# A hybrid SSD and forgetting-attention block: h forms read from a float32 copy in memory, the softplus chain moved behind later slab pairs, the output gate in eight 1024-column steps

## The chip, the cores and the metric

The kernel runs on one core of a Trainium2 chip. Its five engines run their own instruction streams: TensorE (PE; PEld is its weight load), VectorE (DVE), ScalarE (ACT), GpSimd (POOL) and SyncE (SP), which here only issues DMAs. The metric is the device time of one launch in microseconds, as the median of several runs; lower is better.

## What is computed

One layer of a decoder trunk, sequence 1024, width 1024, in float32. What matters here, cut from the reference:

```python
ada = jax.nn.silu(c) @ w_ada + b_ada
shift, scale, gate = jnp.split(ada, 3, axis=-1)
h = _rmsnorm(x, norm_w) * (1.0 + scale) + shift
proj = jnp.einsum("bsd,de->bse", h, w_in)          # 8472 columns
z_ssm, xbc, dt_raw, q, k, v, z_att, f_logit, g_logit = jnp.split(proj, offsets, axis=-1)
dt = jax.nn.softplus(dt_raw + dt_bias)             # used by the SSD branch
a_cs = jnp.cumsum(dt * -exp(a_log), chunkwise)     # used by the SSD branch
f_cum = jnp.cumsum(log_sigmoid(f_logit + b_f))     # used by the attention branch
merged = g_ssm * (y_ssm @ w_proj_ssm) + g_att * (y_att @ w_proj_att)
x = x + gate * (merged @ w_out)
return _rmsnorm(x, final_norm_w)
```

## The kernel before

Every large product is made in three passes: each operand is split into a high and a low part (`split`, lines 98 and 99: a cast on ScalarE and a subtraction on VectorE), and TensorE adds high x high, high x low and low x high in PSUM. The work runs in stages.

1. **h.** x is normalised, transposed on TensorE and scaled by the adaLN columns into `xa` (ScalarE, line 301), 16 halves of 128x512. Each half is split into `hh` and `hl` (lines 302, 303). The adaLN columns come from 8 steps `ada_cols`, whose sums are VectorE's. The weights `w_ada`, x and the first units of the projection are loaded by SyncE's queue in that time.
2. **First slabs.** Three gate slabs, then `v_slab(0)` (four units of `w_v0`; its evacuation also copies the 24 columns of dt and f into `tmp`), then one more gate slab, `gate_slab(3)`.
3. **t forms.** Later slabs are projected in pairs by a seven-product (Strassen-like) scheme, `c_pair`. Four of the products take sums of h rather than h. `t_forms(k)`, k = 0 to 3, makes these: it adds `hh` and `hl` back to float32 (line 436, four adds for each k), makes four differences (lines 437 to 440) and splits them into `tha`, `tla`, `thb`, `tlb`.
4. **Softplus chain.** `dt_chain` turns `tmp` into dt and the logs of the forget gates; `ssm_sums` makes the running sums for the SSD branch. Their results go to memory (`f_scr`, `a_scr`, `e_scr`) and are read in stages 6 and 7.
5. **Pairs.** A loop over `PAIRS`, 19 slab pairs of 7 x 12 matmuls. `WPREP[n]` says what is prepared ahead of pair n for the end of the kernel: sums of the weights of the two output projections (`w_sums`, 'ps', 'pa', 'o') and the output gate. The gate is `silu(c) @ w` by VectorE: `out_gate` multiplies blocks of weights by columns of silu(c) and adds them in `gb` (lines 558 and 561), `gate_sum` adds over partitions with a matmul against ones (line 570).
6. **SSD** with the remaining slabs as filler, 7. **attention**, 8. **output projections** and the last norm.

The code's order isn't the engines' order: a scheduler sorts each engine's instructions by priorities and a simulated timeline when the kernel is built, and then each engine runs its list strictly in order. Buffers come from pools with few slots: `wr` (raw weights, 4 slots), `pe` (4), `sh` (4), and `ev` (4 slots of 128x1028, shared by nearly all that goes to memory).

Of the kernel before, what the change touches and what calls it, by code (L numbers as in the profile page):

```python
# [31 lines left out]
P = 128  # L32
# [19 lines left out]
WPREP = {0: [('ps', 0)], 2: [('ps', 1)], 3: [('ps', 2)], 6: [('ps', 3), ('pa', 0)], 8: [('pa', 1)], 10: [('pa', 2), ('g', 0)], 12: [('pa', 3), ('g', 2), ('g', 3)], 11: [('g', 1)], 13: [('G', 0)], 15: [('o', 0)], 16: [('o', 1)], 17: [('o', 2)], 18: [('o', 3)]}  # L52
# [13 lines left out]
def build(ctx, tc, t):  # L66
# [98 lines left out]
    m_scr = {}  # L165
    z_scr = [dram.tile([P, S], F32, name=f"z_scr{j}") for j in range(8)]
# [31 lines left out]
    with tc.tile_pool(name="st", bufs=1, side="right") as st, \  # L198
# [95 lines left out]
        def h_half(k, hf):  # L294
# [6 lines left out]
            A.activation(out=xa, in_=tp, func=AF.Identity, scale=av[:, k:k + 1], bias=sv[:, k:k + 1])  # L301
            A.copy(out=hh[k][:, fs], in_=xa)  # L302
# [24 lines left out]
    ed = const.tile([P, NC, 8], F32, name="ed")  # L327

# [27 lines left out]
    with tc.tile_pool(name="pa", bufs=1, side="right") as pa, \  # L356
            tc.tile_pool(name="pap", bufs=1, space=PSUM) as pap:

        def dt_chain(dtf, tmp):
# [21 lines left out]
            lf = tmp[:, 192:256].rearrange("p (h c) -> p h c", h=8)  # L381
            pre = tmp[:, 256:320].rearrange("p (h c) -> p h c", h=8)
# [3 lines left out]
            for c in range(1, 8):  # L386
                V.tensor_tensor(out=pre[:, :, c:c + 1], in0=pre[:, :, c - 1:c], in1=lf[:, :, c - 1:c], op=ALU.add)
            ps = pap.tile([P, 512], F32, tag="pp", bufs=5, name="pp")
            PE.matmul(ps[0:64, 0:P], lhsT=tmp[:, 192:256], rhs=tri, start=True, stop=False)
            PE.matmul(ps[0:64, 0:P], lhsT=tmp[:, 256:320], rhs=ones, start=False, stop=True)  # L390
            ft = tmp[0:64, 320:320 + P]
            V.tensor_copy(out=ft, in_=ps[0:64, 0:P])
            SP.dma_start(out=f_scr, in_=ft)

            V.tensor_copy(out=dt, in_=v[:, :, 0:16])
# [35 lines left out]
        def t_forms(k):  # L431
            th1, tl1, th2, tl2 = (pa.tile([P, S], F32R, name=f"t{n}{k}") for n in ("ha", "la", "hb", "lb"))
            b11, b12, b21, b22 = (pe_tile() for _ in range(4))
            lo, hi = slice(0, 512), slice(512, 1024)
            for b, kk, hs, eng in ((b11, k, lo, V), (b12, k, hi, V), (b22, k + 4, hi, V), (b21, k + 4, lo, V)):
                eng.tensor_tensor(out=b, in0=f32(hh[kk][:, hs]), in1=f32(hl[kk][:, hs]), op=ALU.add)
# [812 lines left out]
```

## Time and profile before

| what | value |
|---|---|
| median of 3 runs | 1234.88 us (1232.15 to 1235.67) |
| profiled execution: its time | 1229.0 us |
| profiled execution: its span | 1227.2 us |
| busy share of PE, PEld, DVE, ACT, POOL | 95%, 79%, 79%, 51%, 7% |
| mean granted TensorE clock | 0.992 |
| DMA | 219.67 MB, mean 179 GB/s |

The profiled execution is one execution; its time is 0.5% under the median of the others, and its span lies 1.8 us under its own time. A busy share is an average over the stages. TensorE is nearly always busy, so what costs time is where its row has a gap, and what ended that gap.

### The profile page before, as it was taken

What the parts mean: (1) busy time and instruction counts of PE and PEld (TensorE: products, weight loads), DVE (VectorE), ACT (ScalarE), POOL (GpSimd) and SP (SyncE); (2) the same over time, 40 slices, a digit from 0 to 9 for tenths busy, and PEclk for the clock granted to TensorE, in tenths of its full rate; (3) what the DMA queues carried; (4) which work ended last, traced back from release to release, by engine and by line L of the source; (5) the groups of instructions that cost most, each with busy time, mean ns of one, the idle gap of its engine ahead of it and who ended that gap; (6) DMA issues with size and microseconds to landing.
All of it is one profiled execution on the core that took longest, in us unless ns stands there. A gap on an engine that the chain in (4) does not pass through costs nothing.

```text
span 1227.2 us, 18314 instructions
## 1 busy us (share of the span) xinstructions
PE 1162.5 (95%) x6206; PEld 975.1 (79%) x6206; DVE 969.8 (79%) x1990; ACT 626.2 (51%) x1252; POOL 87.2 (7%) x152
## 2 busy tenths in 40 slices
PE   4999899999999999999999989999988998999997
PEld 3797688778877788998888768888877886788875
DVE  6879687887987785589999987664677968989967
ACT  5555344353442344777776633453456654454455
POOL 2000000000000000000000002222322220000001
PEclk9999999999999999999999989999999999999999
DMA  8442442655384756546646658422246526955333
GB/s 350 178 155 98 165 164 79 229 188 190 115 291 167 243 206 223 207 134 205 207 149 199 205 185 304 157 88 89 87 162 208 182 77 239 334 181 180 103 95 146
DMA packets 104122, 219.67 MB, mean 179 GB/s; under 512 B 11818, under 2 KB 19420, under 8 KB 103004
## 3 DMA queue, kind: packets, MB, share of 16 engines
q1 hardware_dynamic: 104028, 218.50, 52.8%
q8 instruction: 49, 0.80, 0.3%
q14 instruction: 45, 0.37, 0.1%
HBM read 154.85 MB, written 63.61 MB: 178 GB/s over the span
## 4 chain that ended last, share of the span: by engine, by line
PE 71%; DVE 14%; DMA 8%; issue 3%; ACT 3%; POOL 0%; SPq 0%; POOLq 0%; DVEq 0%; ACTq 0%
PE pp L492 6%; PE pp L495 6%; PE pp L494 6%; PE pv L1054 4%; PE mm L492 4%; PE mm L494 4%; PE mm L495 4%; PE lg L1023 3%; PE mm L112 3%; PE mm L111 3%; PE mm L113 3%; DMA ab<-a_scr 2%; PE tp L1044 2%; PE mm L908 2%; PE mm L906 2%
## 5 line engine op out<-in xcount | busy, mean ns | idle before, releaser
L98 ACT CAST wh<-wr 128x512 fp32r<-128x512 f32 (+1 forms) x214 | 130.4, 620 | 159.6 <-PE mm L494 27.9
L99 DVE TENSOR_TENSOR wl<-wr,wh 128x512 fp32r<-128x512 f32 (+1 forms) x214 | 145.8, 689 | 47.3 <-ACT wh L98 46.1
L112 PE MATMUL mm<-hl,wh 128*128 128x512 f32 x288 | 116.9, 406 | 0.0
L111 PE MATMUL mm<-hh,wh 128*128 128x512 f32 x288 | 115.5, 406 | 0.1
L113 PE MATMUL mm<-hh,wl 128*128 128x512 f32 x288 | 114.7, 399 | 0.0
L138 PE MATMUL mm<-wh,hl 128*128 128x256 f32 (+1 forms) x256 | 73.7, 289 | 0.0
L136 PE MATMUL mm<-wh,hh 128*128 128x256 f32 (+1 forms) x256 | 73.2, 288 | 0.0
L137 PE MATMUL mm<-wl,hh 128*128 128x256 f32 (+1 forms) x256 | 73.1, 286 | 0.0
L1029 ACT ACTIVATE pr<-pr,sm 128x1024 f32<-128x1024 f32 (+3 forms) x64 | 50.0, 781 | 44.9 <-DVE sm L1028 38.0
L1047 ACT CAST pth<-tp 128x512 fp32r<-128x512 f32 (+1 forms) x80 | 42.4, 542 | 52.7 <-PE tp L1044 44.1
L1024 DVE CUSTOM_DVE_ANT_0 pr<-lg,fb 128x512 f32<-128x512 f32 (+1 forms) x96 | 51.6, 552 | 17.8 <-PE lg L1023 12.2
L112 PEld LDWEIGHTS mm<-hl,wh 128*128 128x128 f32 x288 | 54.9, 191 | 10.8 <-DVE hl L303 0.9
L111 PEld LDWEIGHTS mm<-hh,wh 128*128 128x128 f32 x288 | 54.5, 191 | 10.9 <-ACT hh L302 0.9
L113 PEld LDWEIGHTS mm<-hh,wl 128*128 128x128 f32 x288 | 54.8, 190 | 10.1
L683 ACT ACTIVATE ab<-ab,acs 128x128 f32<-128x128 f32 x128 | 41.0, 391 | 36.5 <-DMA ab<-a_scr 32.7
L1032 POOL TENSOR_SCALAR pr<-pr,sm 128x1024 f32<-128x1024 f32 (+3 forms) x64 | 52.0, 813 | 83.1 <-DVE sm L1031 65.9
L1048 DVE TENSOR_TENSOR ptl<-tp,pth 128x512 fp32r<-128x512 f32 (+1 forms) x80 | 49.9, 631 | 10.0 <-ACT pth L1047 9.7
L789 POOL TENSOR_TENSOR rc<-rc,mhalf 128x8 f32<-128x8 f32 x1 | 1.6, 1647 | 703.9 <-DVE rc L787 703.9
L1054 PE MATMUL pv<-pth,vh 128*128 128x256 f32 (+1 forms) x160 | 45.2, 282 | 4.9 <-DVE zg L1057 4.0
L98 ACT CAST sh<-sr 128x512 fp32r<-128x512 f32 x57 | 34.0, 620 | 30.3 <-PE pp L494 15.0
L137 PEld LDWEIGHTS mm<-wl,hh 128*128 128x128 f32 x256 | 48.2, 189 | 0.2
L138 PEld LDWEIGHTS mm<-wh,hl 128*128 128x128 f32 x256 | 48.2, 189 | 0.1
(399 smaller groups left out, 3507.6 us busy)
## 6 DMA issues: line engine op xcount, KB each, us to landing
wr<-w_c SPq DMA_DIRECT2D x116, 256.0 KB, 3.4
wa<-w_ada SPq DMA_DIRECT2D x8, 1024.0 KB, 11.4
g_scr<-gt SPq DMA_DIRECT2D x16, 512.0 KB, 4.1
ab<-a_scr SPq DMA_DIRECT2D x32, 256.0 KB, 3.6
gt<-g_scr SPq DMA_DIRECT2D x32, 256.0 KB, 3.9
wr<-w_ps SPq DMA_DIRECT2D x28, 256.0 KB, 2.9
wr<-w_pa SPq DMA_DIRECT2D x28, 256.0 KB, 2.8
wr<-so SPq DMA_DIRECT2D x28, 256.0 KB, 2.7
```

What stands on the lines that cost most here:

```text
L98: A.copy(out=hi[:, :n], in_=raw[:, :n])
L99: eng.tensor_tensor(out=lo[:, :n], in0=raw[:, :n], in1=f32(hi[:, :n]), op=ALU.subtract)
L111: PE.matmul(ps, lhsT=hi[:, cs], rhs=xh[k][:, hs], start=(k == 0), stop=False)
L112: PE.matmul(ps, lhsT=hi[:, cs], rhs=xl[k][:, hs], start=False, stop=False)
L113: PE.matmul(ps, lhsT=lo[:, cs], rhs=xh[k][:, hs], start=False, stop=(k == 7))
L136: PE.matmul(o, lhsT=xh[k][:, ts], rhs=hi[:, cs], start=(k == 0), stop=False)
L137: PE.matmul(o, lhsT=xh[k][:, ts], rhs=lo[:, cs], start=False, stop=False)
L138: PE.matmul(o, lhsT=xl[k][:, ts], rhs=hi[:, cs], start=False, stop=(k == 7))
L492: PE.matmul(ps, lhsT=f[0][:, w], rhs=xh[:, hs], start=(first and k == 0), stop=False, skip_group_check=True)
L494: PE.matmul(ps, lhsT=f[0][:, w], rhs=xl[:, hs], start=False, stop=False, skip_group_check=True)
L495: PE.matmul(ps, lhsT=f[1][:, w], rhs=xh[:, hs], start=False, stop=(k == 3), skip_group_check=True)
L1054: PE.matmul(pv[:, o0:256], lhsT=x[kb // 4][:, kb % 4, vs], rhs=y[:, d:d + m], start=(kb == 0 and i == 0), stop=(kb == 2 * qq + 1 and i == 2))
```

## The change

Six edits. The 16 halves of `xa` are also stored to memory (`h_scr`); `t_forms` loads its four float32 blocks from there rather than adding `hh` and `hl`, for odd k into slots of `sh` rather than `pe`. `gate_slab(3)` now stands ahead of `t_forms`. The 24 columns in `tmp` go to memory (`d_scr`), come back at pair 2, where `dt_chain` now is; its two matmuls (`f_sums`) and `ssm_sums` stand at pair 5. The first `ps` step of `WPREP` moves from pair 0 to pair 1. `out_gate` takes whole rows of 1024 columns, two of the eight k each time, in place of 256 columns for all eight. A constant tile `fl` holds what `tmp` held of the f part (and later `rc`).

```diff
-WPREP = {0: [('ps', 0)], 2: [('ps', 1)], 3: [('ps', 2)], 6: [('ps', 3), ('pa', 0)], 8: [('pa', 1)], 10: [('pa', 2), ('g', 0)], 12: [('pa', 3), ('g', 2), ('g', 3)], 11: [('g', 1)], 13: [('G', 0)], 15: [('o', 0)], 16: [('o', 1)], 17: [('o', 2)], 18: [('o', 3)]}
+WPREP = {1: [('ps', 0)], 2: [('ps', 1)], 3: [('ps', 2)], 6: [('ps', 3), ('pa', 0)], 8: [('pa', 1)], 10: [('pa', 2), ('g', 0)], 12: [('pa', 3), ('g', 2), ('g', 3)], 11: [('g', 1)], 13: [('G', 0)], 15: [('o', 0)], 16: [('o', 1)], 17: [('o', 2)], 18: [('o', 3)]}
...
+    h_scr = [dram.tile([P, S], F32, name=f"h_scr{k}") for k in range(NK)]
+    d_scr = dram.tile([P, 192], F32, name="d_scr")
...
             A.activation(out=xa, in_=tp, func=AF.Identity, scale=av[:, k:k + 1], bias=sv[:, k:k + 1])
+            SP.dma_start(out=h_scr[k][:, fs], in_=xa)
             A.copy(out=hh[k][:, fs], in_=xa)
             V.tensor_tensor(out=hl[k][:, fs], in0=xa, in1=f32(hh[k][:, fs]), op=ALU.subtract)
...
+    fl = const.tile([P, P], F32, name="fl")
...
-            lf = tmp[:, 192:256].rearrange("p (h c) -> p h c", h=8)
-            pre = tmp[:, 256:320].rearrange("p (h c) -> p h c", h=8)
+            lf = fl[:, 0:64].rearrange("p (h c) -> p h c", h=8)
+            pre = fl[:, 64:128].rearrange("p (h c) -> p h c", h=8)
...
+            V.tensor_copy(out=dt, in_=v[:, :, 0:16])
+
+        def f_sums():
             ps = pap.tile([P, 512], F32, tag="pp", bufs=5, name="pp")
-            PE.matmul(ps[0:64, 0:P], lhsT=tmp[:, 192:256], rhs=tri, start=True, stop=False)
-            PE.matmul(ps[0:64, 0:P], lhsT=tmp[:, 256:320], rhs=ones, start=False, stop=True)
-            ft = tmp[0:64, 320:320 + P]
-            V.tensor_copy(out=ft, in_=ps[0:64, 0:P])
-            SP.dma_start(out=f_scr, in_=ft)
-
-            V.tensor_copy(out=dt, in_=v[:, :, 0:16])
+            PE.matmul(ps[0:64, 0:P], lhsT=fl[:, 0:64], rhs=tri, start=True, stop=False)
+            PE.matmul(ps[0:64, 0:P], lhsT=fl[:, 64:128], rhs=ones, start=False, stop=True)
+            V.tensor_copy(out=fl[0:64], in_=ps[0:64, 0:P])
+            SP.dma_start(out=f_scr, in_=fl[0:64])
 
...
         def t_forms(k):
             th1, tl1, th2, tl2 = (pa.tile([P, S], F32R, name=f"t{n}{k}") for n in ("ha", "la", "hb", "lb"))
-            b11, b12, b21, b22 = (pe_tile() for _ in range(4))
+            b11, b12, b21, b22 = (pe_tile() if k % 2 == 0 else pa.tile([P, 512], F32, tag="sh", bufs=SB[1], name="sb")
+                                  for _ in range(4))
             lo, hi = slice(0, 512), slice(512, 1024)
-            for b, kk, hs, eng in ((b11, k, lo, V), (b12, k, hi, V), (b22, k + 4, hi, V), (b21, k + 4, lo, V)):
-                eng.tensor_tensor(out=b, in0=f32(hh[kk][:, hs]), in1=f32(hl[kk][:, hs]), op=ALU.add)
+            for b, kk, hs in ((b12, k, hi), (b11, k, lo), (b22, k + 4, hi), (b21, k + 4, lo)):
+                SP.dma_start(out=b, in_=h_scr[kk][:, hs])
             V.tensor_tensor(out=b11, in0=b12, in1=b11, op=ALU.subtract)
             V.tensor_tensor(out=b12, in0=b22, in1=b12, op=ALU.subtract)
             V.tensor_tensor(out=b22, in0=b22, in1=b11, op=ALU.subtract)
...
             gb = ev("gb") if gb is None else gb
-            gc = slice(g * 256, (g + 1) * 256)
-            for hf in range(2):
-                wa = ev("wga")[:, :1024].rearrange("p (k c) -> p k c", k=4)
-                SP.dma_start(out=wa, in_=t["w_gate"][g, hf])
-                for kk in range(4):
-                    k = hf * 4 + kk
-                    if k == 0:
-                        V.tensor_scalar(out=gb[:, gc], in0=wa[:, kk, :], scalar1=cols[:, k:k + 1], scalar2=None,
-                                        op0=ALU.mult)
-                    else:
-                        V.scalar_tensor_tensor(out=gb[:, gc], in0=wa[:, kk, :], scalar=cols[:, k:k + 1],
-                                               in1=gb[:, gc], op0=ALU.mult, op1=ALU.add)
+            for k in (2 * g, 2 * g + 1):
+                wa = ev("wga")[:, :D]
+                SP.dma_start(out=wa, in_=t["w_gate"][k])
+                if k == 0:
+                    V.tensor_scalar(out=gb[:, :D], in0=wa, scalar1=cols[:, k:k + 1], scalar2=None, op0=ALU.mult)
+                else:
+                    V.scalar_tensor_tensor(out=gb[:, :D], in0=wa, scalar=cols[:, k:k + 1], in1=gb[:, :D],
+                                           op0=ALU.mult, op1=ALU.add)
             return gb
...
         tmp = ev("tmp")
         dtf = tmp[:, 0:192].rearrange("p (c n) -> p c n", n=24)
         v_slab(0, dtf)
+        SP.dma_start(out=d_scr, in_=tmp[:, 0:192])
+        gate_slab(3)
         for k in range(4):
             t_forms(k)
-        gate_slab(3)
-        dt_chain(dtf, tmp)
-        ssm_sums()
         gb = None
         for n, (sa, sb) in enumerate(PAIRS):
+            if n == 2:
+                tmp = ev("tmp")
+                SP.dma_start(out=tmp[:, 0:192], in_=d_scr)
+                dt_chain(tmp[:, 0:192].rearrange("p (c n) -> p c n", n=24), tmp)
+            if n == 5:
+                f_sums()
+                ssm_sums()
             for wn, p in WPREP.get(n, ()):
                 if wn == "g":
...
-        rc = const.tile([P, 8], F32, name="rc")
+        rc = fl[:, 0:8]
...
-        "w_gate": _ada_groups(i["w_ada"][:, 2048:3072].reshape(1024, 1, 1024)),
+        "w_gate": np.ascontiguousarray(i["w_ada"][:, 2048:3072].reshape(8, 128, 1024)),
```

How the engines' lists move, at the three places that the prediction speaks of.

VectorE, from the last halves of h on (line 303, now 306). Before, the adds of line 436 follow at once, four for each k:

```order
L303 TENSOR_TENSOR hl_245<-xa,hh_237 128x512 x2
L303 TENSOR_TENSOR hl_246<-xa,hh_238 128x512 x2
L436 TENSOR_TENSOR pe<-hh_231,hl_239 128x512 x2
L436 TENSOR_TENSOR pe<-hh_235,hl_243 128x512 x2
L437 TENSOR_TENSOR pe<-pe 128x512
L438 TENSOR_TENSOR pe<-pe 128x512
L99 TENSOR_TENSOR wl<-wr,wh 128x560
L439 TENSOR_TENSOR pe<-pe 128x512
L99 TENSOR_TENSOR wl<-wr,wh 128x512
L99 TENSOR_TENSOR tla_1063<-pe,tha_1062 128x512
L440 TENSOR_TENSOR pe<-pe 128x512
L436 TENSOR_TENSOR pe<-hh_232,hl_240 128x512
```

Now (lines 442 to 445 are the four differences; `sb` are the slots of `sh`):

```order
L306 TENSOR_TENSOR hl_254<-xa,hh_246 128x512 x2
L306 TENSOR_TENSOR hl_255<-xa,hh_247 128x512 x2
L442 TENSOR_TENSOR pe<-pe 128x512
L99 TENSOR_TENSOR wl<-wr,wh 128x560
L443 TENSOR_TENSOR pe<-pe 128x512
L99 TENSOR_TENSOR wl<-wr,wh 128x512
L444 TENSOR_TENSOR pe<-pe 128x512
L442 TENSOR_TENSOR sb<-sb 128x512
L99 TENSOR_TENSOR tla_1156<-pe,tha_1155 128x512
L445 TENSOR_TENSOR pe<-pe 128x512
L99 TENSOR_TENSOR tla_1156<-pe,tha_1155 128x512
L443 TENSOR_TENSOR sb<-sb 128x512
```

The adds are gone, and the first instruction after h is a difference of two loaded blocks.

SyncE's queue at the same place. Before (line 85: units of a slab; 579: `w_ps`; 183: a gate slab to memory):

```order
L85 DMA wr<-w_v 128x560 x4
L85 DMA wr<-w_c 128x512 x2
L579 DMA wr<-w_ps 128x512
L183 DMA g_scr_95<-gt 128x1024
L579 DMA wr<-w_ps 128x512
L183 DMA g_scr_96<-gt 128x1024
L579 DMA wr<-w_ps 128x512
L183 DMA g_scr_97<-gt 128x1024
L579 DMA wr<-w_ps 128x512
```

Now (line 304: the stores of xa; 441: the loads of `t_forms`; 463: raw weights of a pair):

```order
L85 DMA wr<-w_c 128x512
L463 DMA wr<-w_c 128x512
L304 DMA h_scr_184<-xa 128x512 x2
L304 DMA h_scr_185<-xa 128x512 x2
L304 DMA h_scr_186<-xa 128x512 x2
L441 DMA pe<-h_scr_179 128x512 x2
L441 DMA pe<-h_scr_183 128x512 x2
L441 DMA sb<-h_scr_180 128x512 x2
L441 DMA sb<-h_scr_184 128x512 x2
L185 DMA g_scr_95<-gt 128x1024
L463 DMA wr<-w_c 128x512
L185 DMA g_scr_96<-gt 128x1024
```

The last stores of h and the first eight loads stand ahead of the gate slabs' stores, and pair 0's raw weights ahead of `w_ps`. The first of the loads into `pe` waits, in the built program, for the stores of h to have completed.

TensorE at the gate's sum (line 570, now 571). Before, the first of its two matmuls stands in the middle of a pair, and the second 50 matmuls later:

```order
L494 MATMUL pp<-tlb_1137,wh 128x512
L495 MATMUL pp<-thb_1136,wl 128x512
L570 MATMUL pp<-gb,ones 128x512
L492 MATMUL pp<-tha_1062,sh 128x512
L494 MATMUL pp<-tla_1063,sh 128x512
```

Now both stand side by side, at the end of a pair and ahead of the next:

```order
L497 MATMUL pp<-hh_247,sh 128x512
L499 MATMUL pp<-hl_255,sh 128x512
L500 MATMUL pp<-hh_247,sl 128x512
L571 MATMUL pp<-gb,ones 128x512
L571 MATMUL mm<-gb,ones 128x512
L497 MATMUL mm<-hh_240,wh 128x512
```

From the start of TensorE's list, the two stood as its 1551st and 1601st matmul, and now as its 1563rd and 1564th; each column of `gb` is now complete only after the last of the eight steps.

## Rows read from the trace of the kernel before

**Rows 1.** The page: busy time by engine, and the chain by engine.
```profile
PE 1162.5 (95%) x6206; PEld 975.1 (79%) x6206; DVE 969.8 (79%) x1990; ACT 626.2 (51%) x1252; POOL 87.2 (7%) x152
...
PE 71%; DVE 14%; DMA 8%; issue 3%; ACT 3%; POOL 0%; SPq 0%; POOLq 0%; DVEq 0%; ACTq 0%
```

**Rows 2.** Windows 70:110 and 110:134.
```profile
core 0: us, PE busy (x) PEld busy (x) DVE busy (x) ACT busy (x) POOL busy (x), PEclk, DMA share, GB/s
70.00:110.00 40.00, 40.00 (x259) 37.15 (x258) 38.88 (x73) 21.32 (x41) 0.00 (x0) 1.00 0.49 165
110.00:134.00 24.00, 19.19 (x80) 14.21 (x79) 20.57 (x45) 9.45 (x17) 0.00 (x0) 1.00 0.48 163
```

**Rows 3.** TensorE in order of time, 110 to 140: its waits.
```profile
120.88 0.50 PE L492 MATMUL mm<-tha,wh 128*128 128x512 f32 x1 [1.46 <-ACT pe L506]
...
124.88 0.50 PE L492 MATMUL mm<-thb,wh 128*128 128x512 f32 x1 [0.96 <-ACT pe L509]
...
128.50 0.50 PE L492 MATMUL mm<-hh,sh 128*128 128x512 f32 x1 [0.57 <-DVE mm L513]
...
133.83 0.49 PE L405 MATMUL pp<-a,tri 128*128 128x128 f32 x2 [1.67 <-DVE a L400]
```

**Rows 4.** Window 60:125, line 436 alone (VectorE busy).
```profile
60.00:125.00 65.00, 10.37 (x16) 1.00 0.36 122
```

**Rows 5.** VectorE in order of time, at two places.
```profile
345.62 0.47 DVE L561 SCALAR_TENSOR_TENSOR gb<-wga,cols,gb 128x256 f32<-128x256 f32 x1
346.01 0.69 DVE L473 TENSOR_TENSOR sr<-wr 128x512 f32<-128x512 f32 x1
346.62 0.48 DVE L561 SCALAR_TENSOR_TENSOR gb<-wga,cols,gb 128x256 f32<-128x256 f32 x1
...
166.38 2.47 DVE L541 SCALAR_TENSOR_TENSOR cv<-xp,cols,cv 128x1024 f32<-128x1024 f32 x2
168.77 0.68 DVE L99 TENSOR_TENSOR wl<-wr,wh 128x512 fp32r<-128x512 f32 x1
```

**Rows 6.** ScalarE in order of time, the last xa.
```profile
68.23 0.78 ACT L301 ACTIVATE xa<-tp,sv,av 128x512 f32<-128x512 f32 x1 [1.10 <-PE tp L298]
```

**Rows 7.** DMA issues: count, KB each, median us to landing.
```profile
wr<-w_c SPq DMA_DIRECT2D x116, 256.0 KB, 3.4
...
sps<-sr SPq DMA_DIRECT2D x12, 256.0 KB, 3.3
...
wr<-w_v SPq DMA_DIRECT2D x4, 280.0 KB, 7.2
```

**Rows 8.** TensorE in order of time, gate slab 3 begins.
```profile
97.06 0.39 PE L111 MATMUL mm<-hh,wh 128*128 128x512 f32 x1
```

**Rows 9.** Window 100:145, tile tmp alone (PE, PEld, VectorE, ScalarE busy).
```profile
100.00:145.00 45.00, 0.87 (x4) 0.38 (x4) 8.36 (x28) 0.36 (x1) 1.00 0.44 150
```

**Rows 10.** Window 150:350, columns as in rows 2.
```profile
150.00:350.00 200.00, 198.58 (x858) 160.58 (x857) 162.94 (x237) 87.11 (x149) 0.00 (x0) 1.00 0.51 172
```

**Rows 11.** TensorE in order of time, 360 to 410: its waits.
```profile
365.72 0.50 PE L492 MATMUL pp<-thb,wh 128*128 128x512 f32 x1 [0.96 <-ACT pe L509]
...
377.97 0.54 PE L492 MATMUL pp<-hh,wh 128*128 128x512 f32 x1 [2.82 <-DVE zt L525]
...
401.18 0.50 PE L492 MATMUL pp<-hh,wh 128*128 128x512 f32 x1 [1.19 <-ACT wh L98]
```

**Rows 12.** Windows 378:380 and 380:382, columns as in rows 2.
```profile
378.00:380.00 2.00, 2.00 (x5) 1.58 (x6) 2.00 (x5) 0.53 (x2) 0.00 (x0) 0.57 0.13 53
380.00:382.00 2.00, 2.00 (x7) 1.56 (x6) 0.90 (x2) 0.00 (x0) 0.00 (x0) 0.57 0.86 344
```

**Rows 13.** Window 335:385, tile gb alone (PE, PEld, VectorE busy).
```profile
335.00:385.00 50.00, 1.02 (x2) 0.38 (x2) 14.41 (x32) 0.97 0.73 256
```

**Rows 14.** SyncE in order of time, w_v0 units; window 34:36.
```profile
34.81 6.38 SPq L85 DMA_DIRECT2D wr<-w_v  x4
...
34.00:36.00 2.00, 2.00 (x12) 1.66 (x10) 1.88 (x6) 0.00 (x0) 0.00 (x0) 1.00 1.05 407
```

More of the change, by code (lines that the diff above doesn't have):

```diff
@@ L1194, in _ada_blocks @@
     return np.ascontiguousarray(w.reshape(8, 128, 2, 8, 128).transpose(3, 1, 0, 2, 4)).reshape(8, 128, 8, 256)
-def _ada_groups(w):
-    m = w.shape[1]
-    return np.ascontiguousarray(w.reshape(2, 4, 128, m, 4, 256).transpose(4, 0, 2, 1, 3, 5)).reshape(4, 2, 128, 4, 256 * m)
 def _t_units(w, c):
```

## The prediction

> **What bounds the kernel now.** Read the page first: TensorE is busy for 95% of the span, and the chain that ended last runs through it for 71% [rows 1]. TensorE's work isn't touched, so time can be won or lost only where TensorE has a gap, or by a lower clock behind a gap. Next read TensorE's waits in order of time. Two places bear on this change. Between 110 and 134 us it waits four times, 1.46 + 0.96 + 0.57 + 1.67 = 4.66 us [rows 3]. The windows say why: in the 40 us before, VectorE was busy for 38.9, and TensorE for all 40, so VectorE fell behind while TensorE still had v_slab(0) and gate_slab(3) to do, and in 110:134 TensorE ran dry [rows 2]. The last of the four is different in kind: TensorE's list has the ssm_sums matmuls there, and stands until VectorE comes to the `a` that they read. The second place is the gate: waits of 0.96, 2.82 and 1.19 us [rows 11], and behind the long one a granted clock of 0.57 for 4 us, in which 5 + 7 matmuls ran [rows 12]; at the 0.23 us from matmul to matmul that holds elsewhere 17 would have fitted, so some 1.7 us more (4 x 0.43) are lost. [...]
>
> **h forms.** Sixteen additions go, 10.37 us of busy time [rows 4]; back to back, a 512-wide operation starts 0.60 to 0.61 us after the one before (346.01 to 346.62 [rows 5]), so 16 x 0.605 = 9.7 us of VectorE's list. The price is at the start. The last xa ends at 68.23 + 0.78 = 69.0 us [rows 6]. Its store is issued then, and a 256 KB store takes 3.3 us to land [rows 7]: 72.3. Only then can the first load be issued, 3.4 us [rows 7]: 75.7, against 70.5 for the first addition before. VectorE idles about 5 us of the 9.7 away, and TensorE doesn't feel it, since v_slab(0) runs until 97. Who is late next? gate_slab(3), at 97.06 [rows 8]. Its second unit is split on VectorE behind 33 operations of 0.605 us and 8 small ones of 0.1 in the new list: 75.7 + 20.0 + 0.8 = 96.5. It is needed after 12 matmuls, at 97.1 + 12 x 0.23 = 99.8. There are 3 us to spare. Behind this, VectorE's list is shorter by the softplus chain, 8.4 us of busy time in 28 operations [rows 9], and by the four sums of 'ps' 0 (2.4 us), which now come after pair 0's first raw weights. Against 5 us lost stand 9.7 + 8.4 less overlap + 2.4 won, some 13 us net, for gaps that sum to 4.66. The fourth gap goes by itself, as ssm_sums moved on. I take all of it: **-4.7 us**, bounds 0 and -4.7.
>
> **The first stage.** The 16 stores stand in SyncE's queue between the loads of w_ada and w_v0. They don't hold up those behind them, since the loads wait for VectorE to free a slot in the same places. But the DMA engines are full there, 1.05 at 407 GB/s in 34:36 [rows 14], and two stores (at about 30 and 32 us) run ahead of the last w_ada and the w_v0 units: 2 x 262 KB at 407 GB/s = 1.3 us. Here VectorE and ScalarE have their own lists in order behind a w_v0 cast, so I pass it on in full: **+1.3 us**, bounds 0 and +2.6 (four stores).
>
> **The chain, later.** The 8.4 us and the few operations of ssm_sums now fall into 165 to 230 us, within a stretch in which VectorE is busy for 163 of 200 us and TensorE for 198.6 [rows 10]. There is room for it on the mean, 37 us, but conv pairs fill VectorE for 20 us at a time, and f_sums and ssm_sums can again stop TensorE's list. `tmp` also holds one of the four `ev` slots there, and its reload waits behind pair 4's raw weights in SyncE's queue. Below: nothing. Above: a gap such as the 1.67 us of `a` plus one of 0.96 [rows 3], +2.6. As the room is wide, I take **+1.0 us**.
>
> **The gate.** Its 32 operations are busy for 14.41 us [rows 13]. Start to start a 256-wide step is 0.39 us (345.62 to 346.01), 28 of them and 4 shorter ones of about 0.26: 12.0 us. A 1024-wide step is 2.39 / 2 = 1.20 (166.38 to 168.77 [rows 5]); seven and one shorter of some 0.7: 9.1. VectorE gains 2.9 us in the stretch where TensorE lost 4.97 in waits and 1.7 in clock, 6.7 together. Working against it: both gate matmuls now stand at one point, at TensorE's 1563rd matmul, where only the first stood at the 1551st; so all eight steps have to be done some 38 matmuls (9 us) earlier than the last of the 32 was, and TensorE stands still until they are. Bounds: -6.7 (all goes), +2 (a new wait like the 2.82 with its clock, 4.5, for 2.5 recovered). The VectorE time is measured, the order isn't; I take half of the 6.7: **-3.3 us**. [...]
>
> The late stages have the same instructions; in attention and output projections even their order is nearly unchanged, so I leave them at zero. The sum against the profiled execution: 1229.0 - 4.7 + 1.3 + 1.0 - 3.3 = 1223.3. That execution lies 5.9 us below the median of the runs shown, so as a median: 1234.9 - 5.7 = **1229.2 us**.
>
> **Rivals.**
> 1. *Both places go wholly*: -4.7 - 6.7 with the first stage and the chain hidden, -11.4: 1223.5. For it: VectorE's list is shorter at both. Against it: the gate's two matmuls side by side.
> 2. *The gain is given back*: the chain's 9 us fall on a full stretch of VectorE and make a gap like the gate's 2.82, the gate keeps its waits: -4.7 + 1.3 + 2.8 + 0 = -0.6: 1234.3. For it: every edit but the first two is only a move of work, and TensorE's 1.4 us idle in 150 to 350 [rows 10] show how little it waited there. It is also the case in which the change does nothing that can be measured.
> 3. *Slower: the loads of h come late.* If they land like the w_v0 units, in 7.2 us [rows 7], since eight are issued at once beside three gate slabs' stores, the first difference is at 79.5, and the second set, which waits for the first's slots, is late by 3.8 again: gate_slab(3)'s second unit is split at 96.5 + 7.6 = 104.1 rather than by 99.8. TensorE stands for 4.3 us, with 1.7 of clock behind it, and pair 0 finds VectorE as late as before, so nothing of the 4.7 is won: +6.0 + 1.3 + 1.0 = +8.3: 1243. It decides from the point at which the loads eat more than the 3 us to spare. Against it: in 70 to 110 us the DMA engines are half free [rows 2].
>
> **How the numbers follow.** Forecast (-4 to -9): 0.44. Rival 1 (beyond -9): 0.15. Rival 2 (within 3.7 us, 0.3%, about what a measurement of this kernel can tell from no change): 0.27. Rival 3 and other losses: 0.14. So faster 0.59, same 0.27, slower 0.14. The range leaves out the further half of rival 1 and rival 3: 1222.5 to 1237.
>
> **What would show it.** Right: no TensorE wait between 110 and 140; VectorE idle from 70 to about 75.5, then busy until about 107, and waiting for TensorE by 114; the gate's matmuls adjacent, with less than 3 us of wait around them and no window under 0.9 there. Wrong: a TensorE wait at gate_slab(3) near 100 (rival 3); a wait in 165 to 230 ended by VectorE, or at f_sums or ssm_sums (rival 2); a wait of over 3 us at the gate's matmul; TensorE reaching v_slab(0) more than 2 us later than now. What I can't read from the trace is the SSD stage, whose lists are sorted anew: a shift of 2 to 3 us either way there would move the result across a bound without any of these steps.

## The result, and the profile after

The changed kernel takes 1225.03 us (median of 4, 1224.55 to 1225.91) beside 1235.28 us (median of 4, 1232.15 to 1237.64) for the kernel before: ratio 0.9913, 95% interval 0.9894 to 0.9932, so about 10.3 us faster. Measured a second time beside other kernels it was 1226.72 (6 executions, 1223.80 to 1230.95), ratio 0.9927 (0.9904 to 0.9950). The forecast was 1229.2, that is -5.7; "faster" and the range held, but the time is almost that of the rival by which both places go wholly (1223.5). By the prediction's own division a gain of more than 9 us is that rival's share (0.15), not the forecast's (0.44).

The page of the changed kernel's profiled execution (1224.89 us), to be held against [rows 1]:

```profile
span 1223.2 us, 18391 instructions
...
PE 1162.6 (95%) x6206; PEld 976.3 (80%) x6206; DVE 957.2 (78%) x1950; ACT 626.5 (51%) x1252; POOL 88.3 (7%) x152
...
PE 66%; DVE 15%; DMA 12%; issue 4%; ACT 3%; POOL 1%; SPq 0%; DVEq 0%; POOLq 0%; ACTq 0%
```

TensorE's busy time is as before; the span is 4.0 us shorter than in the profile of before. That this is less than 10.3 comes from the profile of before, as the first experiment shows: that execution took 1229.0 us where the median is 1235, and it lost nothing to the clock in the first stage, where the thirteen other profiles used here lose 1.7 to 5.2 us.

The forecast's first sign, windows 70:110 and 110:134 as in [rows 2]:

```profile
70.00:110.00 40.00, 37.58 (x242) 35.30 (x241) 29.18 (x54) 21.80 (x41) 0.00 (x0) 0.96 0.64 219
110.00:134.00 24.00, 24.00 (x106) 19.56 (x106) 13.45 (x22) 9.40 (x16) 0.00 (x0) 1.00 0.55 189
```

The stretch in which TensorE ran dry is now full, and VectorE is busy for 13.5 of its 24 us. But the window ahead of it is no longer full for TensorE. TensorE in order of time, its two new waits (the bracket holds the wait and what ended it):

```profile
41.70 0.79 PE L112 MATMUL mm<-hl,wh 128*128 128x512 f32 x1 [1.90 <-DVE hl L306]
...
86.03 0.40 PE L136 MATMUL mm<-wh,hh 128*128 128x280 f32 x1 [2.42 <-DVE tmp L348]
```

and VectorE around the second of them:

```profile
77.09 0.69 DVE L442 TENSOR_TENSOR pe<-pe 128x512 f32<-128x512 f32 x1 [4.72 <-DMA pe<-h_scr]
77.70 0.73 DVE L99 TENSOR_TENSOR wl<-wr,wh 128x560 fp32r<-128x560 f32 x1
...
81.58 0.69 DVE L442 TENSOR_TENSOR sb<-sb 128x512 f32<-128x512 f32 x1 [1.33 <-DMA sb<-h_scr]
...
85.20 0.68 DVE L99 TENSOR_TENSOR tla<-sb,tha 128x512 fp32r<-128x512 f32 x1
85.80 0.27 DVE L348 COPY tmp<-mm 128x24 f32<-128x24 f32 x2
```

The first difference of the h forms waits 4.72 us for its load and comes at 77.09, the second set waits another 1.33; then VectorE works the forms off back to back, and the copy of v_slab(0)'s 24 columns into tmp, queued behind them, runs at 85.80. TensorE's next matmul writes an `mm` buffer, and what ended its wait of 2.42 us is that copy. The windows over it show the price of the wait, and a second one behind it (the granted clock is the third number from the right):

```profile
84.00:86.00 2.00, 0.00 (x0) 0.00 (x0) 2.00 (x7) 1.02 (x3) 0.00 (x0) 1.00 1.05 421
86.00:88.00 2.00, 1.97 (x11) 1.97 (x12) 2.00 (x6) 0.62 (x1) 0.00 (x0) 0.72 1.02 401
88.00:90.00 2.00, 2.00 (x11) 2.00 (x10) 2.00 (x4) 0.00 (x0) 0.00 (x0) 0.50 1.05 400
```

TensorE had stood for 2.42 us; behind that the granted clock was 0.72 and 0.50 in these windows, and 0.93 in 90:92.

At the gate, against [rows 11]: one wait of 0.26 where there was one of 2.82 (the wait of 0.96 ahead of it stays), no window under 1.00 up to 410 us, and a wait at 450 us that is new:

```profile
371.08 1.12 PE L571 MATMUL pp<-gb,ones 128*128 128x512 f32 x2 [0.26 <-DVE gb L562]
372.04 1.02 PE L571 MATMUL mm<-gb,ones 128*128 128x512 f32 x2
...
450.40 0.50 PE L497 MATMUL pp<-thb,wh 128*128 128x512 f32 x1 [1.96 <-ACT pe L514]
```

The last place is one the prediction left at zero, the end of the SSD stage. TensorE in order of time, the sums over `sacc`, then the two waits that lead to attention:

```profile
724.38 0.95 PE L791 MATMUL sp<-ones,sacc 128*128 128x1 f32 x8
727.31 0.27 PE L798 MATMUL sp<-ident,fl 128*8 128x128 f32 x1 [1.99 <-POOL fl L796]
729.09 0.77 PE L1030 MATMUL lg<-kh,qh 128*128 128x512 f32 x1 [1.50 <-DMA fb<-f_scr]
```

In the kernel before a wait of 2.18 us for VectorE's `sacc` stands ahead of the first of these rows; here it is gone.

### The profile page after: what moved, and what is told of

It is laid out like the page before. It is cut to its first block, busy times and chain, and to the rows that moved or that the text cites. A ratio compares the mean times of both kernels' runs of the same rounds, so it can differ in the third digit from the quotient of the medians.

```text
span 1223.2 us, 18391 instructions
## 1 busy us (share of the span) xinstructions
PE 1162.6 (95%) x6206; PEld 976.3 (80%) x6206; DVE 957.2 (78%) x1950; ACT 626.5 (51%) x1252; POOL 88.3 (7%) x152
## 4 chain that ended last, share of the span: by engine, by line
PE 66%; DVE 15%; DMA 12%; issue 4%; ACT 3%; POOL 1%; SPq 0%; DVEq 0%; POOLq 0%; ACTq 0%
PE pp L497 4%; PE pp L499 4%; PE pp L500 4%; PE pv L1061 4%; PE mm L497 3%; PE mm L499 3%; PE mm L112 3%; PE mm L500 3%; PE mm L113 3%; PE lg L1030 3%; PE mm L111 3%; DMA ab<-a_scr 3%; PE tp L1051 2%; PE mm L915 2%; PE mm L913 2%
## 5 line engine op out<-in xcount | busy, mean ns | idle before, releaser
L113 PEld LDWEIGHTS mm<-hh,wl 128*128 128x128 f32 x288 | 54.9, 191 | 10.3
L136 PEld LDWEIGHTS mm<-wh,hh 128*128 128x128 f32 x256 | 48.8, 191 | 2.8 <-DVE tmp L348 2.6
## 6 DMA issues: line engine op xcount, KB each, us to landing
wa<-w_ada SPq DMA_DIRECT2D x8, 1024.0 KB, 11.4
```

The lines of the kernel that those rows point to most:

```text
L113: PE.matmul(ps, lhsT=lo[:, cs], rhs=xh[k][:, hs], start=False, stop=(k == 7))
L136: PE.matmul(o, lhsT=xh[k][:, ts], rhs=hi[:, cs], start=(k == 0), stop=False)
```

## The experiments

Each kernel was timed beside the kernel before on the same chip. Ratios are to that:

| kernel | us, median (executions) | ratio | 95% interval |
|---|---|---|---|
| before again (e1_same) | 1235.13 (12) | 1.0004 | 0.9989 to 1.0019 |
| gate alone (e2_gate) | 1228.13 (7) | 0.9946 | 0.9926 to 0.9966 |
| late chain alone (e3_chain) | 1235.65 (12) | 1.0007 | 0.9989 to 1.0026 |
| h forms alone (e4_forms) | 1237.94 (12) | 1.0026 | 1.0010 to 1.0042 |
| forms + chain (f1_nogate) | 1232.74 (12) | 0.9966 | 0.9948 to 0.9983 |
| chain + gate (f2_noforms) | 1229.66 (6) | 0.9941 | 0.9918 to 0.9963 |
| forms + gate (f3_nochain) | 1231.94 (12) | 0.9961 | 0.9946 to 0.9975 |
| all three, again (g1_after) | 1226.72 (6) | 0.9927 | 0.9904 to 0.9950 |
| all, tmp on ScalarE (f4_actcopy) | 1218.86 (6) | 0.9865 | 0.9839 to 0.9891 |
| all, six xa buffers (g2_xa) | 1223.33 (6) | 0.9897 | 0.9875 to 0.9920 |
| all, gate in short steps (g3_short) | 1224.42 (6) | 0.9906 | 0.9884 to 0.9928 |
| all, both mends (g4_both) | 1223.86 (6) | 0.9900 | 0.9876 to 0.9924 |

The second table says where TensorE lost time in one profile of each. It is worked out from the windows, cut at 10 us: a window's length less PE's busy time is idle, its length times (1 - granted clock) is lost to the clock, and each entry is the sum of both. These losses are good to 1 or 2 us, no better: idle time at the lower clock counts twice, and what is left without them between gate_slab(3) and attention, where the work is the same, is 610 to 613 us. Columns: start of v_slab(0); its length; then the losses from gate_slab(3) to 140 us, 140 to 300, 300 to 410 (the gate), 410 to 600, 600 to attention's first matmul; and from there to the end, in us.

| profile | v_slab(0) starts | long | to 140 | to 300 | to 410 | to 600 | to attention | rest |
|---|---|---|---|---|---|---|---|---|
| before | 70.8 | 26.3 | 4.8 | 1.4 | 6.8 | 0.0 | 12.5 | 493.4 |
| e1_same | 73.2 | 26.3 | 5.2 | 1.4 | 7.5 | 0.4 | 13.5 | 495.3 |
| e2_gate | 72.2 | 26.3 | 5.0 | 1.4 | 1.7 | 0.8 | 9.1 | 496.0 |
| e3_chain | 72.5 | 26.3 | 0.5 | 6.3 | 8.2 | 0.3 | 14.4 | 495.6 |
| e4_forms | 73.5 | 28.3 | 0.0 | 2.6 | 6.8 | 5.0 | 16.0 | 494.0 |
| f1_nogate | 72.6 | 30.8 | 0.0 | 1.2 | 5.7 | 1.1 | 13.5 | 494.7 |
| f2_noforms | 72.9 | 26.3 | 0.3 | 6.4 | 9.4 | 2.6 | 8.8 | 491.7 |
| f3_nochain | 73.2 | 28.5 | 0.0 | 4.2 | 1.2 | 6.4 | 9.1 | 497.9 |
| after | 72.8 | 30.3 | 0.0 | 1.3 | 1.2 | 3.3 | 8.6 | 494.1 |
| g1_after | 73.2 | 28.3 | 0.0 | 1.1 | 1.2 | 5.2 | 8.9 | 494.7 |
| f4_actcopy | 73.9 | 27.2 | 0.0 | 1.4 | 1.2 | 4.5 | 10.3 | 492.3 |
| g2_xa | 73.9 | 28.4 | 0.0 | 1.0 | 1.2 | 2.2 | 8.4 | 494.6 |
| g3_short | 73.2 | 30.5 | 0.0 | 1.1 | 2.1 | 0.6 | 9.0 | 496.6 |
| g4_both | 73.7 | 26.8 | 0.0 | 1.5 | 1.2 | 2.3 | 8.7 | 496.5 |

**The kernel before, again.** No edit.

> The kernel before, unchanged, against itself, to see how far its executions differ and what their granted clock is. Theory: the profiled execution of before (1229.0 us, clock 0.992) was one of its better ones, and the others lose some 6 us to the clock in the places where TensorE waits; then the executions range over some 1229 to 1238 us, and the clock falls with the time (0.985 or so at 1236). Rival: the clock is the same in all, 0.992 within 0.001, and the 6 us are lost in waits, by transfers that land later. Ratio 1.00 within 0.3% by both.

The theory held in the main. Thirty executions of before beside these kernels ran from 1231.50 us at a mean clock of 0.992 to 1241.02 at 0.984, and the time falls as the clock rises (correlation -0.82). But a line through the thirty gives 0.76 us for 0.001 of clock, where 0.001 of 1235 is 1.24, so the clock isn't all of it. The profile here (1237.0 us, clock 0.987) loses 3.4 us to the clock ahead of v_slab(0), the one of before nothing; v_slab(0) begins 2.4 us later, out of 8.1 us between the two spans. So the base of the prediction's sum, 1229.0, was a lucky execution; the forecast didn't suffer, as it took differences and set them on the median. One profile against one profile would have shown -4.0 instead of -10.3.

**The gate alone.** The kernel before with the diff's part in `out_gate`, and nothing else:

```diff
-            for hf in range(2):
-                wa = ev("wga")[:, :1024].rearrange("p (k c) -> p k c", k=4)
...
+            for k in (2 * g, 2 * g + 1):
+                wa = ev("wga")[:, :D]
```

> Only the output gate in eight 1024-column steps, with its matmuls side by side; the additions, the chain and the order of the rest as before. Theory: the wait of 2.82 us and the clock behind it go also here, since they hang on the gate's own VectorE operations and place: 3 to 7 us faster than before, no window under 0.9 near the gate. Rival: the wait goes in the changed kernel because pairs 0 to 10 run with more room on VectorE; then the gate by itself gives under 1.5 us, and a wait of 2 us or more stands at the gate's matmuls.

6.7 us faster by the ratio: the theory, at its upper end. At the gate TensorE loses 1.7 instead of 6.8 to 7.5, which is 5 to 6 us; the rest comes at the end of the SSD stage (9.1 against 12.5 to 13.5).

**The late chain alone.** The kernel before, with

```diff
-        dt_chain(dtf, tmp)
-        ssm_sums()
...
+            if n == 2:
...
+                dt_chain(tmp[:, 0:192].rearrange("p (c n) -> p c n", n=24), tmp)
+            if n == 5:
+                f_sums()
+                ssm_sums()
```

> Only the softplus chain and its products put off (chain at pair 2, sums at pair 5, with the copy of its input in memory); the 16 additions, the first stage and the gate as before. Theory: TensorE's four waits between 110 and 134 us (4.66 us) are a backlog on VectorE of that length, and taking the 8.4 us of the chain from it is enough: they shrink to under 1.5 us, the start is as before (v_slab(0) begins at 70.8 us and has no wait of 2.4 us), and the kernel is 3 to 5 us faster, without the copies of h. Rival: the additions are needed for it; then 2 us or more of the waits stay and the gain is under 2 us, a single wait (1.67 us at ssm_sums) less.

Half of the theory held. The waits at 110 to 140 us shrink from 5.2 to 0.5, without the copies of h; but nothing is won, since a new gap takes their place. TensorE in order of time:

```profile
214.56 0.43 PE L395 MATMUL pp<-ones,fl 128*64 128x128 f32 x2 [0.78 <-DVE fl L389]
...
217.34 0.49 PE L407 MATMUL pp<-a,tri 128*128 128x128 f32 x2 [2.35 <-DVE a L402]
...
224.22 0.50 PE L494 MATMUL pp<-hh,wh 128*128 128x512 f32 x1 [3.14 <-ACT pe L505]
```

6.3 us of them, where the prediction's second rival had 2.8: the chain's work and the conv pair's stand on VectorE together, and f_sums and ssm_sums stop TensorE's list.

**The h forms alone.** The kernel before with the h stores, the loads in `t_forms` and gate_slab(3) ahead of them:

```diff
+            SP.dma_start(out=h_scr[k][:, fs], in_=xa)
...
+            for b, kk, hs in ((b12, k, hi), (b11, k, lo), (b22, k + 4, hi), (b21, k + 4, lo)):
+                SP.dma_start(out=b, in_=h_scr[kk][:, hs])
```

> Only the h forms from the copy in memory, with gate_slab(3) ahead of them as in the changed kernel; chain, sums and gate as before. Theory: the copies cost TensorE 2 us in the first stage, then 2.4 us and some 2 us of half clock at v_slab(0), where its copy into tmp stands behind forms that wait for loads; VectorE still has the chain at 110 to 134 us, and saves 9.7 of 18 us there: the four waits shrink to about 1.5 us. Together -3 + 6 = 3 us slower, or no change within 0.3%. Rival: the copies are what closes the gaps, and the gain at 110 to 134 is whole: 3 us or more faster.

3.2 us slower by the ratio. The gaps to 140 us are gone altogether, more than the theory had, and are paid back: 2.0 us at v_slab(0), 1.2 in 140 to 300, 4 to 5 more in 410 to 600, and 2.5 to 3.5 more at the end of the SSD stage. So neither of the two edits to the head of the kernel helps by itself. Two waits of this kernel, at the copy into tmp and at the unchanged gate:

```profile
86.21 0.39 PE L136 MATMUL mm<-wh,hh 128*128 128x280 f32 x1 [1.90 <-DVE tmp L346]
...
379.07 0.79 PE L495 MATMUL pp<-hh,wh 128*128 128x512 f32 x1 [3.44 <-DVE zt L528]
```

**Forms and chain together, gate undone.** The changed kernel with the old `out_gate`.

> The changed kernel with its gate edit undone (gate in 32 steps of 256 columns; h forms from memory and the late chain stay). Theory: the forms and the late chain need each other: 5 us of waits at 110 to 140 us go, and the gap that the late chain alone opened at 214 to 224 us (5 us) does not come, since VectorE is some 8 us ahead there; v_slab(0) loses its 4 us. The gate's wait of 2.8 us and its half clock are back: 1231 to 1233 us, 3 to 4 us faster than before. Rival: forms and chain have nothing to do with each other, their single results add up (+2.6 and +0.3), and the kernel is 3 us slower than before, 1238 us.

The theory in time: -4.2 us by the ratio, where the single results would add up to +4. With the gate's -6.7 that makes -10.9, about what the changed kernel gains. The gap at 214 to 224 us is gone. Counted from gate_slab(3)'s first matmul, VectorE has the `a` that ssm_sums multiplies at 217.0 - 98.8 = 118.2 us with the chain alone, and at 113.8 here and in the changed kernel (216.9 - 103.1): 4.4 us earlier. The theory's reason, a VectorE that is ahead by the additions, isn't what the traces show. In the 50 us that begin 10 us after that matmul, VectorE is idle for some 20 us with the chain alone and for 19 in the changed kernel, so a delay by the additions would have been made up before the sums come (TensorE, PEld, VectorE, ScalarE, POOL busy; first e3_chain, then the changed kernel):

```profile
108.77:158.77 50.00, 49.53 (x215) 39.88 (x214) 30.12 (x51) 19.84 (x36) 0.00 (x0) 1.00 0.51 163
113.10:163.10 50.00, 50.00 (x219) 40.75 (x218) 30.86 (x50) 19.88 (x35) 0.00 (x0) 1.00 0.63 210
```

And the 113.8 is the same in all seven profiles with the forms and the late chain, though v_slab(0) takes from 0.6 to 4.5 us more than 26.3 in them. What differs is the order of the lists: the first matmul of `f_sums` stands 494 places behind gate_slab(3)'s first with the chain alone and 434 in those seven, and VectorE's first `cv` operation comes after 61 us there and after 55 here. What in the forms' edit makes the order was not tried. Nor was the move of the first 'ps' step to pair 1 by itself: this kernel has it, the two single experiments don't.

**Chain and gate, forms undone.** The changed kernel with the additions, and `t_forms` ahead of gate_slab(3), as before.

> The changed kernel with its h forms undone (additions, and forms ahead of gate_slab(3), as before; late chain and gate in 1024-column steps stay). Theory: v_slab(0) has no wait and takes 26.3 us again (4 us won), but VectorE is later by the additions when the sums come, and TensorE waits 4 to 6 us between 210 and 228 us: 1228 to 1230 us, slower than the changed kernel by 3 to 5 us. Rival: the gate in fewer steps or the moved weight sums make room by themselves, no gap near 214, and the kernel is as fast as the changed one or up to 4 us faster.

The theory in time (1229.66) and place. TensorE's three largest waits:

```profile
217.60 0.49 PE L407 MATMUL pp<-a,tri 128*128 128x128 f32 x2 [3.06 <-DVE a L402]
...
224.65 0.50 PE L494 MATMUL pp<-hh,wh 128*128 128x512 f32 x1 [3.31 <-ACT pe L505]
...
377.54 2.08 PE L568 MATMUL pp<-gb,ones 128*128 128x512 f32 x2 [6.01 <-DVE gb L559]
```

The late `a` is there, and with it as long a gap as with the chain alone (6.4 and 6.3 us lost in 140 to 300), so the moved 'ps' step doesn't close it. VectorE misses the gate too: 9.4 us lost in 300 to 410, more than before. Yet the kernel is 7.3 us faster than before by the ratio. With the loss at the gate as it is, that comes from behind it: 8.8 us are lost from 600 us to attention, against 12.5 to 13.5, and the rest takes 491.7 us instead of 493.4 and 495.3.

**Forms and gate, without the late chain.** The kernel before with the two edits above; the chain and its sums stand ahead of the pairs.

> The changed kernel without the late chain (chain and sums ahead of the pairs, weight sums as before; h forms from memory and gate stay). Theory: as the forms alone (1237.9 us) less the gate's 6.7 us: 1231 us; waits at v_slab(0) 2 us, none at 110 to 140, and still slower than the changed kernel by about 6 us. Rival: the late chain gives nothing once the forms are there, and this is within 2 us of the changed kernel.

1231.94 us, and the theory's picture. The late chain, together with the 'ps' step that moves with it, is worth 4 to 6 us beside the other two (0.9961 against 0.9927 and 0.9913); by itself the chain gives nothing.

**The copy into tmp on ScalarE.** The changed kernel, with one line in `v_slab`:

```diff
-                V.tensor_copy(out=dtf[:, tb:tb + per, :], in_=ps[:, :, 256:280])
+                A.copy(out=dtf[:, tb:tb + per, :], in_=ps[:, :, 256:280])
```

> The changed kernel, but v_slab(0) takes its 24 columns into tmp on ScalarE instead of VectorE. Theory: the wait of 2.42 us at 86 us is a copy that stands on VectorE behind forms that wait for the loads of h, and the clock falls to half behind it; on ScalarE the copy waits for nobody, v_slab(0) takes 26.3 instead of 30.3 us, and the kernel is 3 to 4 us faster than the changed one, 1221 to 1222 us. Rival: what is won there is lost by gate_slab(3) or pair 0, which then meet VectorE with its forms unfinished: a wait of 2 to 4 us between 100 and 125 us and 1225 us as now.

1218.86 us, the lowest median of all. Its interval lies below both of the changed kernel's, and meets those of the two kernels with six xa buffers. TensorE's wait at that place, and ScalarE around it:

```profile
85.58 0.40 PE L136 MATMUL mm<-wh,hh 128*128 128x280 f32 x1 [0.84 <-ACT tmp L348]
```

```profile
84.01 0.64 ACT L346 COPY vt<-mm 128x256 f32<-128x256 f32 x2
84.69 0.62 ACT L98 CAST thb<-pe 128x512 fp32r<-128x512 f32 x1
85.35 0.26 ACT L348 COPY tmp<-mm 128x24 f32<-128x24 f32 x2
```

v_slab(0) takes 27.2 us, with a clock of 1.00. That is 1.1 to 3.1 us less than in the two profiles of the changed kernel; the ratio fell by 6 to 8 us. The rest isn't shown: the profiled execution was the slowest of its six (1223.89 at a mean clock of 0.990; four lie at 1218.4 to 1218.9, at 0.989 to 0.992), and its stages behind v_slab(0) are like those of the changed kernel within 2.5 us.

**Six xa buffers.** The changed kernel with

```diff
-            xa = st.tile([P, 512], F32, tag="xa", bufs=4, name="xa")
+            xa = st.tile([P, 512], F32, tag="xa", bufs=6, name="xa")
```

> The changed kernel with six xa buffers instead of four, so that no xa waits until the store of the one four ahead has landed. Theory: the first stage pays for the stores by this wait (1.82 us of ScalarE and 1.90 us of TensorE at 41 us); without it v_slab(0) begins 1 to 2 us earlier and the kernel is 1 to 2 us faster. Rival: the stores cost the stage its share of the DMA engines, as the prediction had it (+1.3 us); then another wait takes its place and the time is the same within 0.5 us.

The rival for the first stage. ScalarE's waits in the changed kernel, window 20:72 (engine, line, what for: total, times, longest), two of its rows:

```profile
ACT xa L303 <- DMA h_scr<-xa: 1.8, 1, 1.8
ACT xa L303 <- DVE sv L294: 1.4, 2, 1.1
```

and the second of these with six buffers, where there is no row for the store any more:

```profile
ACT xa L303 <- DVE sv L294: 12.0, 4, 5.3
```

TensorE's 1.90 us at 41 us are gone too, but v_slab(0) begins at 73.9 us, no earlier than in the changed kernel (72.8 and 73.2): ScalarE's wait for the columns of w_ada takes the place, a wait that the kernel before has too (10.3 us in its profile). By the medians the kernel is 1.7 to 3.4 us faster all the same, but the intervals overlap (0.9875 to 0.9920 against 0.9894 to 0.9932 and 0.9904 to 0.9950). Its profile has attention at 726.2 us instead of 729.1 and 729.8. Against the first, 1.9 us of that lie in v_slab(0); against the second, 3.0 in 410 to 600; none in the first stage.

**The gate's steps cut in four.** The changed kernel, with each step of the gate as

```diff
+                for c0 in range(0, D, 256):
+                    gc = slice(c0, c0 + 256)
...
+                        V.scalar_tensor_tensor(out=gb[:, gc], in0=wa[:, gc], scalar=cols[:, k:k + 1],
...
```

> The changed kernel with each 1024-column step of the gate cut into four operations of 256 columns, in the same place and on the same eight loads: 32 operations again, and the order of loads and products as changed. Theory: half of the gate's 7 us is the fixed part of 24 more operations on VectorE (2.9 us), and the gap at the gate comes back in part: 2 to 4 us slower than the changed kernel. Rival: only the order counts (all steps done ahead of both matmuls, and the later stages sorted anew); then it is within 1 us of the changed kernel.

The rival: 32 short operations in the changed order are as fast (1224.42) as eight long ones (1225.03 and 1226.72), within the noise. At the gate itself 2.1 us are lost instead of 1.2, so the short operations cost 0.9 us there. VectorE in order of time, first the kernel before (its second profile), then this one:

```profile
375.80 0.88 DVE L561 SCALAR_TENSOR_TENSOR gb<-wga,cols,gb 128x256 f32<-128x256 f32 x2
376.59 0.69 DVE L476 TENSOR_TENSOR sr<-wr,sr 128x512 f32<-128x512 f32 x1
377.19 0.88 DVE L561 SCALAR_TENSOR_TENSOR gb<-wga,cols,gb 128x256 f32<-128x256 f32 x2
378.06 0.69 DVE L99 TENSOR_TENSOR sl<-sr,sh 128x512 fp32r<-128x512 f32 x1
378.67 1.39 DVE L561 SCALAR_TENSOR_TENSOR gb<-wga,cols,gb 128x256 f32<-128x256 f32 x3
379.98 0.68 DVE L525 SCALAR_TENSOR_TENSOR zt<-zt,pp 128x512 f32<-128x512 f32 x1
```

```profile
368.32 1.66 DVE L565 SCALAR_TENSOR_TENSOR gb<-wga,cols,gb 128x256 f32<-128x256 f32 x4
369.90 0.68 DVE L99 TENSOR_TENSOR wl<-wr,wh 128x512 fp32r<-128x512 f32 x1
370.50 0.68 DVE L530 SCALAR_TENSOR_TENSOR zt<-zt,pp 128x512 f32<-128x512 f32 x1
371.10 0.68 DVE L478 TENSOR_TENSOR sr<-wr 128x512 f32<-128x512 f32 x1
371.70 1.66 DVE L565 SCALAR_TENSOR_TENSOR gb<-wga,cols,gb 128x256 f32<-128x256 f32 x4
373.28 0.68 DVE L530 SCALAR_TENSOR_TENSOR zt<-zt,pp 128x512 f32<-128x512 f32 x1
```

In the kernel before the last twelve gate operations stand at 374 to 384 us between the pair's `sl` and `zt`, and TensorE waits 2.76 us for that `zt`. In the changed order all steps are done by 373.4 (371.0 with long ones), since all must be ahead of the first gate matmul. They fall into a stretch in which VectorE waited for the gate's loads anyway (3.9 to 4.6 us).

**Both mends together.** tmp on ScalarE and six xa buffers.

> The changed kernel with both mends: the 24 columns into tmp on ScalarE, and six xa buffers. Theory: they add up, 4 to 6 us and 1 to 2 us: 1217 to 1220 us, the fastest of all. Rival: the first stage's wait is made up by the clock or by another wait, and this is as fast as the first mend alone, 1219 to 1221 us.

They don't add up: 1223.86 us, between the changed kernel and the first mend alone, whose interval it meets (0.9876 to 0.9924 against 0.9839 to 0.9891). v_slab(0) is 26.8 us long, as the theory wanted. Why the medians lie 5 us apart isn't shown: the two profiled executions took equally long (1223.94 and 1223.89 us). In them attention begins 4.2 us earlier with both mends, and what follows takes 4.2 us longer, of which 2.1 is the clock (9.3 us lost to it against 7.2) and 1.4 idle time. By its median the version to keep is the one with the single line; that it beats the two kernels with six buffers isn't shown by six executions of each.

## Why the prediction was right, and where not

**h forms, -4.7.** The size was right, the gaps to 140 us went from 5.2 to 0, and so was the timetable: VectorE idle until 77.09 (forecast 75.7), gate_slab(3) not starved, no third rival. The reason was incomplete. The late chain closes these gaps by itself to 0.5 (e3_chain). What the forms are needed for is the place to which the chain moves, and there the traces show another order of the lists rather than a VectorE that is ahead (see forms and chain together).

**"TensorE doesn't feel it, since v_slab(0) runs until 97."** This step failed. v_slab(0) feels VectorE through eight 24-column copies of 0.18 us each, which the prediction didn't count among what is queued behind the late loads. In the seven profiles with the h forms and the copy on VectorE v_slab(0) takes 28.3 to 30.8 us, 29.3 in the mean, against 26.3: +3.0 us that no term held. On ScalarE the copy costs 0.6 to 0.9.

**First stage, +1.3.** The sign holds, the size isn't shown: v_slab(0) begins at 73.2 in the mean of seven profiles with stores and four buffers, and at 72.3 in five without stores, +0.9. But the five alone range from 70.8 to 73.2, and at the same loss to the clock there is next to no difference (3.4 us: 73.3 in the mean of six with stores, 73.2 in the one without; 5.1 us: 72.8, and 72.5 and 72.9). What is clear is TensorE's idle time there, 18.6 to 19.2 us without and 19.4 to 20.1 with stores: +0.7. The prediction's own sign of being wrong, v_slab(0) more than 2 us later than in the profile of before, was reached (2.0 and 2.4 us), but by the unchanged kernel too (2.4, e1_same). The wait of ScalarE for an xa whose store hasn't landed was not foreseen, but isn't what sets the start (g2_xa).

**The chain, +1.0.** With the forms nothing (1.1 to 1.3 us lost in 140 to 300 beside 1.4 before); without them +4.9, beyond the bound of 2.6. The mean room of 37 us of VectorE in 150:350 didn't decide, but the order of the lists around the sums.

**The gate, -3.3.** 7.5 (or 6.8) became 1.2: -5.6 to -6.3, near the bound of -6.7. The prediction's reason was wrong. It counted 2.9 us of VectorE's time for the gain and the early place of both matmuls against it; g3_short shows that the 2.9 us are worth 0.9 at the gate, and the rest of the gain goes with the changed order. Its reading of the lower clock (5 + 7 matmuls in 4 us) counts one matmul in both windows; eight stand 0.43 us apart there instead of 0.23, 1.6 us in all, close to its 1.7. What fewer operations save of VectorE's time is nearly as the rows had it: four 256-wide steps take 1.59 us from start to start and a 1024-wide one 1.20, 0.13 us per operation saved, 3.1 us for 24. It has to be read from start to start, since here each operation starts before the one ahead has ended: one of 512 columns takes 0.69 us, and the next starts 0.60 us after it. The kernel's time depends little on it.

**Late stages, zero.** Wrong, both ways. The SSD stage is sorted anew whenever the gate is: all five profiles without the gate's edit lose 12.5 to 16.0 us from 600 us to attention, and have 2.2 us at `sacc` like this one (TensorE, second profile of before)

```profile
734.99 1.26 PE L784 MATMUL sp<-ones,sacc 128*128 128x1 f32 x8 [2.19 <-DVE sacc L778]
738.24 0.38 PE L791 MATMUL sp<-ident,rc 128*8 128x128 f32 x1 [1.99 <-POOL rc L789]
740.02 0.76 PE L1023 MATMUL lg<-kh,qh 128*128 128x512 f32 x1 [1.40 <-DMA fb<-f_scr]
```

and all nine with it lose 8.4 to 10.3, without the first of these waits: -5.0 in the mean. Against it, 3.3 and 5.2 us are lost in 410 to 600 in the changed kernel, where before lost up to 0.4; which edit does that was not tried. The prediction named this as what it couldn't read, 2 to 3 us either way. That the SSD stage gains with the gate's edit is shown; which of its instructions' places does it was not tried, and the same is open for the part of two experiments (six buffers, tmp on ScalarE) that no edited place explains.

The sum, from e1_same (whose 3.4 us lost to the clock ahead of v_slab(0) are nearer to the changed kernel's 5.2 and 3.4 than the other profile's 0.0) to the mean of the two profiles of the changed kernel: start -0.2, v_slab(0) +3.1, gaps to 140 us -5.2, 140 to 300 -0.2, gate -6.3, 410 to 600 +3.9, SSD -4.8, the rest -0.9: -10.6, beside -11.4 in span and -9.0 to -10.7 by the two ratios. Against the forecast's -5.7 that is 4.9 more: first stage -1.5, v_slab(0) +3.1, h forms -0.5, chain -1.2, gate -3.0, late stages -1.8. So both places went almost wholly, as the rival had it, and the three sizeable terms that no sum held (v_slab(0) +3.1, 410 to 600 +3.9, SSD -4.8) largely cancel (+2.2). That the time stayed within the range is in part luck: with the SSD's term alone it would have left it.

## What to carry to other kernels

When work is put ahead of a queue's other entries, list every small entry behind it, not only the large ones: a copy of 0.18 us held TensorE for 1.9 to 2.6 us. Test parts of a change together as well as alone: here two edits gave nothing clear of noise (+0.9 us) and cost 3.2 us by themselves, and gained 4.2 together (with a smaller move beside them). And where a step on VectorE stops TensorE, ask first what it stands in front of; of the 5 to 6 us won at the gate, fewer and longer operations gave 0.9, their new place the rest.

## What the runs showed of the hardware

Ahead of v_slab(0) the loss by the granted clock is 0.0, 1.7, 3.4 or 5.1 us, give or take 0.1, in all fourteen profiles (windows of 10 us, added up), nothing between, and it differs between executions of one kernel (0.0 and 3.4 for before, 5.2 and 3.4 for the changed one). It isn't the time that is lost there, where TensorE is idle for 19 of 71 us: in the five profiles without stores v_slab(0) begins at 70.8 us with a loss of 0.0, at 72.2 with 1.7, at 73.2 with 3.4, and at 72.5 and 72.9 with 5.1. At v_slab(0) of the changed kernel, where TensorE has no gap but the one wait, nearly all of the loss is time: 1.7 us made the slab 1.6 us longer (30.3 us, 2.42 of them the wait, against 26.3).

At v_slab(0) TensorE's clock fell behind waits of 2.42 us (the changed kernel, to 0.50) and 2.63 (g3_short, 0.94 in the mean of the slab), and not behind 1.89 (g2_xa, 1.00), 1.99 (g1_after, 1.00) and 1.90 (e4_forms, where the 280-column matmuls stand 0.13 us apart ahead of the wait and behind it). But the length of a wait doesn't decide by itself: the waits of 3.06 and 3.31 us in f2_noforms (and of 3.14 in e3_chain) left the clock at 1.00. The windows of f2_noforms around the second of them:

```profile
222.00:224.00 2.00, 0.00 (x0) 0.00 (x0) 1.79 (x9) 0.75 (x3) 0.00 (x0) 1.00 0.97 351
224.00:226.00 2.00, 1.35 (x6) 1.14 (x7) 0.70 (x1) 0.70 (x3) 0.00 (x0) 1.00 1.01 347
```
